# One cost in a scheduling planner: what a one-pass matrix product is reckoned at

## The chip, the cores and the metric

The kernel runs on one core of a Trainium2 chip. The metric is the device time of one execution in microseconds. Before the change the median of three runs was 756.35 us, from 755.69 to 757.19. The profile is of one execution of its own, which took 755.57 us; its trace spans 753.8 us from the first instruction to the last.

The core has five engines that matter here. TensorE (PE) multiplies matrices, and loads the stationary operand in a pipeline beside it (PEld). VectorE (DVE) and ScalarE (ACT) work element by element, GpSimd (POOL) does a few small things, and SyncE (SP) starts the transfers. Each engine takes its instructions strictly in the order in which they were written, so an instruction that waits holds up everything behind it on its engine.

## The reference

One layer of a transformer-like trunk over 512 positions of width 1024, in float32:

```python
h = token_mixer(rmsnorm(x, norm_mix_pre), w_in, b_in, ...) ; x = x + rmsnorm(h, norm_mix_post)
h = memory_cross_attention(rmsnorm(x, ...), rmsnorm(mem, ...), wq, wk, wv, wo) ; x = x + rmsnorm(h, ...)
h = conv_glu_ffn(rmsnorm(x, ...), w_up, conv_w, conv_b, w_down) ; x = x + rmsnorm(h, ...)
```

The token mixer projects the normed rows with w_in and runs four groups of four heads side by side: an mLSTM in chunks, a short causal convolution, a blockwise attention with a position bias, and a gated linear recurrence (HGRN) in chunks. Their outputs are joined and multiplied with w_out. Cross attention reads 256 memory rows. The feed-forward part has 2816 gated channels with a causal convolution of width 3.

## The kernel before

**Arithmetic.** A float32 product is done in one of two ways. Where it feeds a long sum (all projections, the output matrices, the feed-forward part), both operands are split into a high and a low part of type fp32r, and three products are made of one: high by high, high by low, low by high (`three`, L480). These are the one-pass products. Each reads the moving operand once. Small products inside the recurrence and the attentions stay in plain float32; the trace shows two MATMUL records for each of those.

**Splitting.** `stage` loads a weight tile (tile `st`), ScalarE writes the high part `wh`, VectorE the low part `wl`. `split` (L483) does the same for activations. So each weight and each activation passes both of these engines before TensorE can use it.

**The planner.** No instruction order is written by hand. The program below first only records operations; each has an engine, a cost in ns, the buffers that it reads and writes, and a unit. `schedule` (L209) then plays the program through: for every engine it keeps the time at which the engine is free, `est` (L234) gives the earliest time at which a ready operation could start by the costs and by fixed gaps between engines, and of those that could start within 1 ns of the earliest the one with the longest chain of costs behind it (plus a boost) is taken. The order in which the operations are taken is the order in which they are issued (`issue`), and also decides which buffer each gets. So a cost enters twice: in the clock of the plan and in the length of the chains. It has no part in what an instruction does on the chip.

The cost of a TensorE operation comes from `mcost` (L451), summed over its products by `mms` (L457). For one-pass products before the change it is

```python
return max(n, 2 * m) / 2.4 + 2.4
```

where n is the number of columns and m at most 128. That is 215.7 ns at 512 columns and 109.1 ns at 256 and fewer. Plain float32 products, transposes (109 ns, `tpose`) and the narrow products of `pair` (L473) have prices of their own.

**The stages**, in order of time: loading and norming x; the projection of the mixer with the HGRN, mLSTM and attention groups woven into it; the memory projections; w_mix_out; cross attention; the feed-forward part up (`w_ffn_in`) and down (`w_ffn_out`). The HGRN group is the function `hgrn_tile` (L793). For each of four tiles of 128 positions and two pairs of heads it makes decay exponents on TensorE (`mats` by `lfh`, `lfl`), exponentiates them on ScalarE (tile `E`), multiplies by query and key on VectorE (tiles `Qt` and `E` again, by `kT`), multiplies these on TensorE, and writes the result through masks into `at` on VectorE (L427). A state per pair of heads (`state`) runs through the four tiles. While that chain goes back and forth, TensorE has projections of the same stage to do, which the planner puts between. In the mLSTM group a row of gates (`ra`, `rg`, `rb`) passes ScalarE and VectorE before TensorE transposes it (`p_322`).

Of the kernel before, what the change touches and what calls it, by code (L numbers as in the profile page):

```python
# [341 lines left out]
def kernel(  # L342
# [108 lines left out]
    def mcost(l, n):  # L451
        m = min(l.size(), P)
        if l.buf.dt == FR:
            return max(n, 2 * m) / 2.4 + 2.4
        return max(n, m) / 0.6 + 4.8

    def mms(o, terms, first=True, last=True, spare=0, n=None, quota=(), after=(), boost=0.0, fifo=None, cold=1):  # L457

        def go():
            for j, (l, r) in enumerate(terms):  # L460
                i = nc.tensor.matmul(o.ap(), l.ap(), r.ap(), start=first and j == 0,  # L461
                                     stop=last and j == len(terms) - 1)
            return i
        return pl.op("PE", cold * sum(mcost(l, n or o.size()) for l, r in terms), go,
                     reads=[v for t in terms for v in t] + ([] if first else [o]), writes=[o], spare=spare, quota=quota, after=after, boost=boost,
                     fifo=fifo if first else None)
# [453 lines left out]
    for h in range(4):  # L920
        with pl.unit():
# [3 lines left out]
            for i in range(NT):  # L925
                n = S - i * P
# [32 lines left out]
    for g in range(2):  # L959
# [6 lines left out]
        for j in range(NT):  # L966
            with pl.unit():
                js, n = slice(j * P, (j + 1) * P), (j + 1) * P
# [342 lines left out]
```

## Time and profile before

| | |
|---|---|
| median of three runs | 756.35 us (755.69 to 757.19) |
| profiled execution, its own time | 755.57 us |
| its span in the trace | 753.8 us |
| TensorE busy | 741.5 us, 98% of the span |
| VectorE busy | 419.4 us, 56% |
| ScalarE busy | 336.8 us, 45% |
| chain that ended last | PE 95%, DVE 2%, DMA 1% |
| HBM traffic | 75.0 MB read, 2.1 MB written |

The chain that ended last is followed back from the last instruction, at each step to what released it. It is TensorE for 95% of the span. Busy time of TensorE overstates its work, because the ends of its pipelined products are modelled; the distance from one start to the next is the better measure. The averages hide that VectorE is busy nearly all of one stretch, and less than half of another.

### The profile page before, as it was taken

How to read it: one execution, taken by the hardware profiler on the slowest of the kernel's cores; microseconds unless marked ns; L12 is line 12 of the kernel's file. 1: busy time of each engine (PE TensorE's matmuls, PEld its weight loads, DVE VectorE, ACT ScalarE, POOL GpSimd, SP SyncE). 2: the span in 40 equal slices, each digit the busy share in tenths (PEclk: the TensorE clock that was granted, in tenths of full speed). 3: DMA queues.
4: the chain of work that ended last, by engine and by line, in shares of the span. 5: the costliest groups of instructions: out<-in, count | busy, mean ns of one | idle time of the engine just before them, and what ended most of it. 6: DMA issues, size and time to landing. Idle time of an engine off the chain costs nothing.

```text
span 753.8 us, 10351 instructions
## 1 busy us (share of the span) xinstructions
PE 741.5 (98%) x4038; PEld 631.1 (84%) x4038; DVE 419.4 (56%) x799; ACT 336.8 (45%) x662; POOL 35.5 (5%) x65
## 2 busy tenths in 40 slices
PE   7999999999999999999999999999999999999996
PEld 6899989998888988989888888888888888888885
DVE  4879948777664745596755443554344453234005
ACT  5794438437663643485635323344232343123002
POOL 3000210030000000000100000000000000000001
PEclk9999999999999999999999999999999999999998
DMA  8801220500515632243232232223132233245002
GB/s 294 299 1 52 79 92 28 197 29 29 197 57 183 221 126 85 85 140 113 90 107 86 82 93 75 85 85 94 46 111 68 73 88 107 84 167 168 1 0 112
DMA packets 24538, 77.78 MB, mean 103 GB/s; under 512 B 2853, under 2 KB 4517, under 8 KB 24489
## 3 DMA queue, kind: packets, MB, share of 16 engines
q1 hardware_dynamic: 24200, 76.53, 30.7%
q8 instruction: 32, 0.52, 0.3%
q0 software_dynamic: 288, 0.59, 0.3%
q14 instruction: 18, 0.14, 0.1%
HBM read 75.00 MB, written 2.11 MB: 102 GB/s over the span
## 4 chain that ended last, share of the span: by engine, by line
PE 95%; DVE 2%; DMA 1%; SPq 0%; issue 0%; ACT 0%; POOL 0%; DVEq 0%; POOLq 0%; ACTq 0%
PE p L461 91%; PE p L478 3%; DMA st<-in_w_in_dram 1%; PE p L473 1%; DVE at L427 1%; DVE Qt L399 1%; SPq L370 0%; DMA cols<-in_cols_dram 0%; DVE E L399 0%; DVE state L411 0%; DVE xs L411 0%; DVE X L411 0%; DVE xTl L399 0%; POOL rr L564 0%; DVEq L1307 0%
## 5 line engine op out<-in xcount | busy, mean ns | idle before, releaser
L461 PE MATMUL p<-xTh,wh 128*128 128x512 f32 (+1 forms) x560 | 211.8, 378 | 0.2 <-ACT xTh L386 0.2
L461 PE MATMUL p<-xTl,wh 128*128 128x512 f32 (+1 forms) x560 | 210.1, 375 | 0.2 <-DVE xTl L399 0.2
L461 PE MATMUL p<-xTh,wl 128*128 128x512 f32 (+1 forms) x560 | 209.6, 374 | 0.0
L399 DVE TENSOR_TENSOR wl<-st,wh 128x1024 fp32r<-128x1024 f32 (+3 forms) x117 | 138.0, 1194 | 89.2 <-ACT wh L386 74.9
L386 ACT ACTIVATE wh<-st 128x1024 fp32r<-128x1024 f32 (+3 forms) x117 | 117.5, 1031 | 57.7 <-DMA st<-in_w_ffn_out_dram 48.4
L461 PEld LDWEIGHTS p<-xTh,wh 128*128 128x128 f32 x560 | 105.4, 188 | 20.2 <-ACT xTh L386 0.5
L461 PEld LDWEIGHTS p<-xTh,wl 128*128 128x128 f32 x560 | 105.2, 188 | 20.5
L461 PEld LDWEIGHTS p<-xTl,wh 128*128 128x128 f32 x560 | 105.2, 188 | 19.8 <-DVE xTl L399 0.5
L461 PE MATMUL p<-wh,hT 128*128 128x512 f32 x288 | 90.1, 393 | 0.0
L411 DVE SCALAR_TENSOR_TENSOR fc<-p,cols,fc 128x511 f32<-128x511 f32 (+1 forms) x44 | 32.8, 748 | 92.7 <-ACT fc L386 92.0
L461 PEld LDWEIGHTS p<-wh,hT 128*128 128x128 f32 x288 | 54.1, 188 | 12.6
L386 ACT ACTIVATE fc<-p,cols 128x512 f32<-128x512 f32 x22 | 15.0, 684 | 97.9 <-PE p L461 97.9
L461 PE MATMUL p<-wh,xTh 128*128 128x256 f32 (+1 forms) x192 | 56.7, 296 | 0.2 <-ACT xTh L386 0.2
L461 PE MATMUL p<-wl,hT 128*128 128x512 f32 x144 | 56.7, 394 | 0.0
L461 PE MATMUL p<-wh,xTl 128*128 128x256 f32 (+1 forms) x192 | 54.1, 282 | 0.4 <-DVE xTl L399 0.4
L461 PE MATMUL p<-wl,xTh 128*128 128x256 f32 (+1 forms) x192 | 54.0, 281 | 0.0
L399 DVE TENSOR_TENSOR pg<-p,gain 128x512 f32<-128x512 f32 x24 | 16.4, 685 | 52.7 <-ACT sq L386 52.7
L386 ACT ACTIVATE sq<-p 128x512 f32<-128x512 f32 x24 | 14.4, 600 | 67.7 <-PE p L461 67.5
L564 POOL TENSOR_TENSOR rr<-rv,mhalf 128x1 f32<-128x1 f32 x26 | 15.0, 576 | 579.9 <-DVE rv L406 575.4
L461 PEld LDWEIGHTS p<-wh,xTh 128*128 128x128 f32 x192 | 36.3, 189 | 0.9 <-ACT xTh L386 0.5
L461 PEld LDWEIGHTS p<-wh,xTl 128*128 128x128 f32 x192 | 36.2, 188 | 0.6 <-DVE xTl L399 0.6
L461 PEld LDWEIGHTS p<-wl,xTh 128*128 128x128 f32 x192 | 36.2, 189 | 0.5
(236 smaller groups left out, 1085.1 us busy)
## 6 DMA issues: line engine op xcount, KB each, us to landing
st<-in_w_ffn_in_dram SPq DMA_DIRECT2D x44, 512.0 KB, 3.6
st<-in_w_in_dram SPq DMA_DIRECT2D x24, 512.0 KB, 4.7
st<-in_w_ffn_out_dram SPq DMA_DIRECT2D x22, 512.0 KB, 3.6
st<-in_w_mix_out_dram SPq DMA_DIRECT2D x8, 512.0 KB, 3.7
st<-in_w_ck_dram SPq DMA_DIRECT2D x4, 512.0 KB, 5.1
st<-in_w_cv_dram SPq DMA_DIRECT2D x4, 512.0 KB, 5.1
st<-in_w_cq_dram SPq DMA_DIRECT2D x4, 512.0 KB, 4.2
X<-in_x_dram SPq DMA_DIRECT2D x4, 512.0 KB, 5.1
```

The costliest lines, as they stand in the source:

```text
L386: return nc.scalar.activation(o.ap(), i.ap(), func, **kw)
L399: return pl.op(eng, c, lambda: e.tensor_tensor(o.ap(), a.ap(), b.ap(), op=op), reads=[a, b], writes=[o], fifo=fifo, boost=boost)
L411: lambda: nc.vector.scalar_tensor_tensor(o.ap(), a.ap(), ap(s), b.ap(), op0=op0, op1=op1),
L427: return pl.op("DVE", dcost(n, True), lambda: nc.vector.copy_predicated(o.ap(), m.ap(), a.ap()), reads=[m, a, o], writes=[o])
L461: i = nc.tensor.matmul(o.ap(), l.ap(), r.ap(), start=first and j == 0, stop=last and j == len(terms) - 1)
L473: i = nc.tensor.matmul(o[hh * 64:hh * 64 + 64].ap(), l.ap(), r.ap(), start=j == 0, stop=j == len(terms) - 1)
L478: return pl.op("PE", 109.0, lambda: nc.tensor.transpose(o.ap(), a.ap(), idn.ap()), reads=[a, idn], writes=[o])
L564: pl.op("Pool", 470.0, lambda: nc.gpsimd.tensor_tensor(r.all.ap(), v.all.ap(), mhalf[:, :1].ap(), op=OP.pow), reads=[v.all, mhalf.all], wr ...
```

## The change

One line of the cost function is replaced. The price of a one-pass product becomes `max(n, 2 * m) * 0.4445 + 3.7`: 231.3 ns at 512 columns, 174.4 at 384, 121.0 at 264, and 117.5 ns at 256 and fewer. All else of the program text is the same, and so are the instructions in kind and number. What differs is their order on each engine, and the buffers.

```diff
     def mcost(l, n):
         m = min(l.size(), P)
         if l.buf.dt == FR:
-            return max(n, 2 * m) / 2.4 + 2.4
+            return max(n, 2 * m) * 0.4445 + 3.7
         return max(n, m) / 0.6 + 4.8
```

In the orders below a name has the buffer's own number first and then its place in the issue order; the first is the same in both programs, the second is not. The first TensorE row that differs is the 47th, a product of the forget gate's projection about 21 us into the run.

TensorE at the end of the HGRN group. `p_249` is the last of the products that take a `Qt` and an `E` from VectorE; `p_113` and `p_116` are a projection for which `wh_108` holds the first half of the weights and `wh_111` the second. Before:

```order
L461 MATMUL p_113_1009<-wh_111_564,xTh_11_63 128x256
L461 MATMUL p_113_1009<-wl_112_578,xTh_11_63 128x256
L461 MATMUL p_113_1009<-wh_111_564,xTl_12_64 128x256
L461 MATMUL p_249_1152<-Qt_248_1132,E_247_1122 128x128 x2
L461 MATMUL p_249_1152<-Qt_248_1132,kT_228_844 128x128
L461 MATMUL p_250_1160<-hqb_88_75,kT_228_844 128x256
```

Now:

```order
L461 MATMUL p_116_1111<-wh_108_457,xTh_11_63 128x256
L461 MATMUL p_116_1111<-wl_109_467,xTh_11_63 128x256
L461 MATMUL p_116_1111<-wh_108_457,xTl_12_64 128x256
L461 MATMUL p_249_1132<-Qt_248_1107,E_247_1091 128x128 x2
L461 MATMUL p_249_1132<-Qt_248_1107,kT_228_823 128x128
L461 MATMUL p_250_1136<-hqb_88_75,kT_228_823 128x256
```

`p_249` has moved ahead of the second half of that projection. Counted over the whole order, 27 one-pass products that stood ahead of it now stand behind it (6 of 512 columns into `p_266`; 12 into `p_113` and 9 into `p_116`, of 256), and 3 plain products of `p_239` have come ahead of it.

VectorE just ahead of the operations that feed `p_249`. Before:

```order
L411 SCALAR_TENSOR_TENSOR state1_105_83<-state1_105_83,gl_219_1044,p_217_996 64x64
L399 TENSOR_TENSOR ho_129_826<-ho_129_826,rr_155_1065 128x256
L399 TENSOR_TENSOR wl_278_1124<-st_276_778,wh_277_780 128x1024
L399 TENSOR_TENSOR Qt_248_1132<-E_247_1122,hqb_88_75 128x128 x3
L399 TENSOR_TENSOR E_247_1122<-E_247_1122,kT_228_844 128x256
```

Now:

```order
L427 COPY_PREDICATED at_230_957<-masks_55_238,p_239_1052 128x256
L411 SCALAR_TENSOR_TENSOR state1_105_83<-state1_105_83,gl_219_1069,p_217_982 64x64 x2
L399 TENSOR_TENSOR hv_91_580<-p_102_818,bbc_92_309 128x256
L444 TENSOR_REDUCE hss_153_1102<-hsq_152_1063 128x4
L399 TENSOR_TENSOR Qt_248_1107<-E_247_1091,hqb_88_75 128x128 x3
L399 TENSOR_TENSOR E_247_1091<-E_247_1091,kT_228_823 128x256
```

From `Qt_137` (the first operation of the second half of HGRN tile 0) to `E_247`, three operations have moved behind (`wl_278`, `ho_129`, `rv_154`) and six have moved ahead (four into `at_230`, `Qp_240`, one into `hv_91`).

TensorE and ScalarE in the mLSTM gates. `p_318` and `p_317` are transposes of the gate inputs, `p_272` and `p_284` projections. TensorE before:

```order
L461 MATMUL p_272_1316<-xTh_11_63,wl_271_1060 128x512
L478 MATMUL p_318_1505<-ident_7_88,mif_286_1483 4x128 x2
L478 MATMUL p_317_1503<-ident_7_88,mif_286_1483 4x128 x2
L461 MATMUL p_284_1592<-xTh_11_63,wh_282_895 128x512
L461 MATMUL p_284_1592<-xTl_12_64,wh_282_895 128x512
```

and now:

```order
L461 MATMUL p_272_1300<-xTh_11_63,wl_271_876 128x512
L461 MATMUL p_284_1582<-xTh_11_63,wh_282_999 128x512
L461 MATMUL p_284_1582<-xTl_12_64,wh_282_999 128x512
L461 MATMUL p_284_1582<-xTh_11_63,wl_283_1168 128x512
L478 MATMUL p_318_1501<-ident_7_88,mif_286_1483 4x128 x2
L478 MATMUL p_317_1499<-ident_7_88,mif_286_1483 4x128 x2
```

Three products have come ahead of the transposes. Behind them 24 products of 512 and 12 of 256 columns stood ahead of `p_322`; now 21 and 6 do. ScalarE there, before:

```order
L386 ACTIVATE pz_267_1589<-p_272_1316,cols_57_254 128x512
L386 ACTIVATE ra_319_1598<-p_318_1505 4x512
L386 ACTIVATE pH_268_1603<-pz_267_1589 128x512
L386 ACTIVATE ra_319_1598<-ra_319_1598 4x512
L386 ACTIVATE hh_258_1611<-pH_268_1603 64x512
L386 ACTIVATE ra_319_1598<-ra_319_1598,one_10_92 4x512
```

and now:

```order
L386 ACTIVATE pz_267_1580<-p_272_1300,cols_57_254 128x512
L386 ACTIVATE pH_268_1597<-pz_267_1580 128x512
L386 ACTIVATE ra_319_1605<-p_318_1501 4x512
L386 ACTIVATE hh_258_1610<-pH_268_1597 64x512
L386 ACTIVATE ra_319_1605<-ra_319_1605 4x512
L386 ACTIVATE hh_258_1610<-pH_268_1597 64x512
L386 ACTIVATE ra_319_1605<-ra_319_1605,one_10_92 4x512
```

The third step of `ra` now has one more copy (`hh_258`) ahead of it. On VectorE the two copies into `hh_258`, which stood between the three later steps of `ra`, have moved ahead of them.

## Rows read from the trace of the kernel before

**Rows 1.** The page: instructions and span, then busy us of each engine.

```profile
span 753.8 us, 10351 instructions
PE 741.5 (98%) x4038; PEld 631.1 (84%) x4038; DVE 419.4 (56%) x799; ACT 336.8 (45%) x662; POOL 35.5 (5%) x65
```

**Rows 2.** Windows: stretch; length; busy of PE, PEld, DVE, ACT, POOL; clock; DMA; GB/s.

```profile
48.00:66.00 18.00, 18.00 (x141) 17.19 (x140) 17.44 (x65) 12.66 (x34) 0.94 (x3) 1.00 0.00 1
66.00:93.00 27.00, 26.68 (x198) 24.87 (x198) 26.63 (x95) 11.12 (x35) 4.34 (x4) 1.00 0.27 90
386.00:747.00 361.00, 361.00 (x1582) 293.37 (x1581) 144.00 (x167) 110.16 (x143) 1.65 (x3) 1.00 0.27 84
```

**Rows 3.** PE timeline, one-pass products: start, length (us), instruction, idle and releaser.

```profile
82.44 0.28 PE L461 MATMUL p<-wl,xTh 128*128 128x256 f32 x1
82.56 0.28 PE L461 MATMUL p<-wh,xTl 128*128 128x256 f32 x1
82.94 0.46 PE L461 MATMUL p<-Qt,E 128*128 128x128 f32 x2
...
384.89 0.49 PE L461 MATMUL p<-xTh,wh 128*128 128x512 f32 x1 [0.25 <-ACT xTh L386]
...
450.27 0.39 PE L461 MATMUL p<-xTh,wh 128*128 128x512 f32 x1
450.50 0.39 PE L461 MATMUL p<-xTl,wh 128*128 128x512 f32 x1
```

**Rows 4.** PE timeline around the last HGRN products.

```profile
66.38 0.28 PE L461 MATMUL p<-wh,xTl 128*128 128x256 f32 x1
66.89 0.49 PE L461 MATMUL p<-Qt,E 128*128 128x128 f32 x2 [0.23 <-DVE E L399]
...
87.24 0.67 PE L461 MATMUL p<-Qt,E 128*128 128x128 f32 x4
...
89.46 0.38 PE L461 MATMUL p<-state,Qp 128*128 128x128 f32 x2
...
90.05 0.36 PE L461 MATMUL p<-wh,xTh 128*128 128x256 f32 x1
```

**Rows 5.** DVE timeline ahead of the last HGRN products.

```profile
84.91 1.22 DVE L399 TENSOR_TENSOR wl<-st,wh 128x1024 fp32r<-128x1024 f32 x1
86.05 0.69 DVE L399 TENSOR_TENSOR Qt<-E,hqb 128x128 f32<-128x128 f32 x3
86.66 0.42 DVE L399 TENSOR_TENSOR E<-E,kT 128x256 f32<-128x256 f32 x1
87.11 1.04 DVE L427 COPY_PREDICATED at<-masks,p 128x128 f32<-128x128 uint8 x4
87.95 0.32 DVE L399 TENSOR_TENSOR Qp<-E,hq 128x128 f32<-128x128 f32 x1
```

**Rows 6.** ACT timeline early in the HGRN group.

```profile
53.56 1.09 ACT L386 ACTIVATE E<-p 128x512 f32<-128x512 f32 x2 [0.98 <-PE p L461]
```

**Rows 7.** Timelines of the mLSTM gates: PE, ACT and DVE.

```profile
132.10 0.28 PE L461 MATMUL p<-wh,xTl 128*128 128x256 f32 x1
132.31 0.22 PE L478 MATMUL p<-ident,ra 4*128 4x4 f32 x1
...
127.25 0.63 ACT L386 ACTIVATE hh<-pH 64x512 fp32r<-64x512 f32 x1
127.90 0.72 ACT L386 ACTIVATE ra<-ra,one 4x512 f32<-4x512 f32 x1
...
129.37 0.41 DVE L423 CAST hh<-pH 64x512 fp32r<-64x512 f32 x1
130.94 0.42 DVE L423 CAST hh<-pH 64x512 fp32r<-64x512 f32 x1
```

**Rows 8.** PE timeline, change from one-pass products to narrow ones and back.

```profile
192.18 0.44 PE L473 MATMUL p<-pt,av 128*64 128x128 f32 x4
192.55 0.50 PE L461 MATMUL p<-hh,hl 128*128 128x512 f32 x1
```

## Prediction

> **What bounds the kernel now.** I read the page's busy times first. TensorE is busy for 741.5 of 753.8 us [rows 1], and the other engines for little more than half or less. So the end is set by the sum of what TensorE has to do and the moments in which it waits. The change leaves its products as they are in kind and number; it can only move waits and the small costs between unlike products.
>
> Next I asked whether the new price is nearer to the truth, in TensorE's timeline. Starts, not lengths, are to be compared, since the ends are modelled. Two one-pass products of 512 columns start at 450.27 and 450.50, 0.23 us apart; two of 256 start at 82.44 and 82.56, 0.12 apart [rows 3]. The new prices are 231.3 and 117.5 ns, the old ones 215.7 and 109.1. The trace thus shows the new price as the true one, within the two digits of the rows, at a clock of 1.00 [rows 2]. A page of the Trainium skill speaks for the old price: "TensorE: Matmul & The Clock Gate", section "Wait — 56ns, not 53.3ns?", gives N/2.4 plus about 2.5 ns from start to start, 215.7 ns at 512 columns. By that figure the old plan kept true time and the new one makes TensorE too slow; the trace does not agree (0.23 us), and I reckon with the trace.
>
> Then I looked by windows for where TensorE waits at all. From 386 to 747 us it is busy in all of 361.00 us [rows 2], so there is nothing to win there. From 48 to 66 us VectorE is busy for 17.44 of 18.00 us and from 66 to 93 us for 26.63 of 27.00 us [rows 2]. That is the HGRN group, and there VectorE and TensorE are both nearly full. TensorE's waits in it are seen in the timeline: 66.38 to 66.89 is 0.51 where a 256-column product takes 0.12, so 0.39 of wait for `E` [rows 4]; 82.56 to 82.94 is 0.38, so 0.26 [rows 3]. The two make 0.65; with several of about 0.1 each I estimate 1.5 us of waits between 66 and 91 us. One other wait is plain, 0.25 us at 384.89 for an `xTh` of ScalarE [rows 3], at a place where the order has not changed, so it stays. All that better ordering can win is therefore some 1.5 us in the HGRN group and a few tenths elsewhere. What it can lose has no such limit.
>
> **The change part by part.** The one thing removed or added is a price. What it moves is read from the orders, what that costs from the rows.
>
> *The end of the HGRN group.* In the old order the last products that need a `Qt` and an `E`, `p_249`, start at 87.24 [rows 4], and the `E` they read is finished on VectorE at 86.66 + 0.42 = 87.08 [rows 5]. So they came just in time: 0.16 us after it, with no slack. In the new order TensorE reaches them with less work behind it: 27 one-pass products now stand behind `p_249`, 6 of 512 and 21 of 256 columns, which is 6 x 0.23 + 21 x 0.12 = 1.38 + 2.52 = 3.90 us. Three plain products of `p_239` have come ahead, from 89.46 to 90.05 = 0.59 us [rows 4]. So TensorE arrives 3.90 - 0.59 = 3.3 us earlier.
>
> Does VectorE deliver earlier by as much? From `Qt_137` to `E_247` its order has lost `wl_278` (84.91 to 86.05, 1.14 us [rows 5]) and two small operations, and gained four copies into `at` (87.11 to 87.95, 0.84 us for four, [rows 5]), a `Qp` and a gating product of `hv`, each of a few tenths. These cancel within about 0.2 us. VectorE is full in this stretch, so it delivers earlier only if it begins earlier. That can be: the first products of the group (`p_134`) have 18 products of 256 columns and two transposes fewer ahead of them, 18 x 0.12 = 2.2 us and some 0.1, about 2.3 us; and early in the group ScalarE waited for TensorE's exponents, 0.98 us at 53.56 [rows 6]. What of the 2.3 reaches the end of the chain no row shows: nothing if VectorE's other work is what fills it, all of it if the exponents were what it lacked. I take 1.0, by the nearest row, ScalarE's 0.98. So the added wait is 3.3 - 1.0 = 2.3, less 0.1 for slack left at 87.08: +2.2 us. Its ends are 3.3 - 2.3 - 0.1 = +0.9, and 3.3 - 0.1 = +3.2. What stands behind the waiting `p_249` on TensorE is the projection into `p_113` and `p_116`, ready long before: work that was used as cover is simply done later and costs the same, so the wait is pure loss. Should VectorE be less late than I think, the 1.5 us of present waits could go as well, which makes the lower end of this term -1.5.
>
> This is also the mechanism that I believe in. The old price let the plan's TensorE run ahead of the real one by 7 in 100. In the plan, then, TensorE arrived at such places too early, and the planner put filling work ahead of them; on the chip this surplus of filler covered VectorE and ScalarE where those are later than their own prices say. With the true price for TensorE alone that surplus is gone.
>
> *The mLSTM gates.* `p_322` starts at 132.31, 0.21 after a product of 256 columns at 132.10 [rows 7], so it already waits 0.09 us: no slack there either. Of its filler, 24 products of 512 and 12 of 256 columns behind the transposes, 21 and 6 are left. The three of 512 now stand before the transposes and move those as well, so measured from the end of `p_272` TensorE comes 6 x 0.12 = 0.7 us earlier. The chain of `ra` has on ScalarE one copy of `hh` more ahead of its third step, 127.25 to 127.90 = 0.65 us, and on VectorE two copies of `hh` fewer between its steps, 0.41 + 0.42 = 0.83 us [rows 7]; the difference is -0.2. The added wait is 0.7 - 0.2 = +0.5 us; the ends are 0, if the copies that moved had already been hidden by a wait for ScalarE, and 0.7 + 0.65 = 1.35 less 0.1, about 1.2, if VectorE gives nothing back.
>
> *Between unlike products.* Narrow products of `pair` cost something at the change to and from one-pass ones. From 192.18 to 192.55 are 0.37 us for four records of 128 columns [rows 8]; at the pace of 512 columns in 0.23 us they would need 4 x 0.058 = 0.23, so a return to one-pass products costs about 0.15. The new order has three more such returns and two fewer entries, which I take at something under 0.1 each: 0.45 - 0.2, some +0.2 us, from 0 to 0.5.
>
> *Elsewhere.* In the attention, in cross attention and in the feed-forward part the distances from producer to consumer are kept or the chains are shorter by an operation. TensorE has no wait to lose there from 386 us on, and other work of its own to do when a chain is late. I take 0, from 0 to 0.5. SyncE's transfers come in nearly the same order; none of the waits above is for one.
>
> The sum is 2.2 + 0.5 + 0.2 + 0 = +2.9 us. Against the profiled execution that is 755.57 + 2.9 = 758.5 us. The median of the runs shown lies 0.8 above that execution, and on it the forecast is 756.35 + 2.9 = 759.2 us.
>
> **The rivals.**
>
> *The start is earlier by all that TensorE gives it* (no change). If VectorE's chain begins 2.3 us sooner and the wait at the gates is hidden by its copies, 0.9 + 0 + 0.1 remain: 757.3 us. For it speaks ScalarE's wait of 0.98 us, which shows that the exponents were late; against it, that VectorE was busy for 97 in 100 of the stretch at the same time [rows 2], so that little of its lateness came from waiting.
>
> *The true price puts the work where it is needed* (faster). With TensorE's clock right the plan sees which products come too late for VectorE's next step, and places them earlier; the 1.5 us of waits in the HGRN group go, the 0.09 at the gates goes, and two fewer entries save some 0.2: 756.35 - 1.8 = 754.6 us. It decides if VectorE starts more than 3.3 us earlier, or if its operations between `Qt_137` and `E_247` wait less than now. For it speaks that the exponents and first products do stand earlier; against it, that VectorE has only 0.37 us of idle time in 66 to 93 us to give, so it must gain before 66 us, where it has 0.56 [rows 2].
>
> *The attention loses its cover too* (slower still). There, too, filler was placed by the false price. If the upper end of the first term holds and 0.5 for the attention, 0.5 for the changes and 0.7 at the gates come to it, the sum is 3.2 + 0.5 + 0.5 + 0.7 = +4.9: 761.3 us. Against it speaks that no wait is seen there now.
>
> *The price tells nothing at all.* The first 46 TensorE instructions and the whole of the down projection stand as before, and TensorE's sum of products is fixed; if waits only change places, the time stays at 756.4. I count it to the first rival.
>
> **How the numbers follow.** A measurement of this kernel can tell about 0.2% from no change, 1.5 us: 754.8 to 757.9. I give my forecast 0.51 (its own range 757.9 to 760.3, from the ends of its first term with the middle of the others), slower still 0.09, the two cases of no change 0.28, faster 0.12. Slower is then 0.51 + 0.09 = 0.60. The range from 755.4 to 761.2 leaves out the faster case and the upper part of the last, not quite 0.2.
>
> **What would show it right or wrong.** In the profile after, TensorE's busy time should be about the same and the span longer by some 3 us. The first step is right if `p_249` starts 0.2 us or less after the end of its `E`, while TensorE's last product before it started over 1 us earlier, and if the operation `E` ends between 1 and 3 us late against TensorE's own work. It is wrong if the whole stretch of HGRN, reckoned by the TensorE work done up to `p_249` and not by the clock, ends with less waiting than before: then VectorE began sooner than I took. The second step is right if `p_322` shows 0.3 us or more of idle time released by VectorE's `ra`, wrong if it follows the product before it without a gap. If there are waits of more than 0.5 us after 140 us, the "elsewhere" is wrong. If the time is below 755 us, the mechanism itself is: the surplus of filler was not what covered VectorE.

## The result and the profile after

The changed kernel takes 761.97 us (median of four runs, 761.11 to 762.78) against 756.02 us of the kernel before on the same chip: 1.0078 times as long, 95% interval 1.0058 to 1.0098. That is 5.95 us slower. The forecast was 759.2 us, with 761.2 as its upper end: the direction is right, the size half of what came. The profiled execution took 761.11 us.

The page and the windows of the changed kernel (stretch; length; busy of PE, PEld, DVE, ACT, POOL; clock; DMA; GB/s), to be held against [rows 1, 2]:

```profile
span 759.3 us, 10365 instructions
PE 746.2 (98%) x4038; PEld 632.2 (83%) x4038; DVE 418.9 (55%) x799; ACT 336.3 (44%) x662; POOL 34.9 (5%) x65
...
48.00:66.00 18.00, 17.85 (x129) 16.09 (x128) 17.62 (x64) 11.00 (x31) 0.94 (x3) 1.00 0.00 1
66.00:93.00 27.00, 26.59 (x198) 24.54 (x198) 25.52 (x91) 10.06 (x30) 4.58 (x5) 1.00 0.27 90
386.00:747.00 361.00, 360.53 (x1589) 292.62 (x1588) 142.30 (x166) 110.14 (x142) 1.65 (x3) 1.00 0.26 83
```

Neither the number of products (4038) nor the clock (1.00) has changed. The span is 5.5 us longer. VectorE and ScalarE do the same work in all. PE's busy time is up by 4.7 us although it does the same products: a modelled end often hides a wait, so busy time is no way to find the loss. What finds it is to take the n-th product of each trace and to subtract its start in the trace before. At the numbers below, the same work lies behind TensorE in both kernels, to within three products of the same size (us against the kernel before; the last two columns are experiments, the first one below and the one with the lower price; in them up to seven 256-column products stand in place of small transposes at number 900):

```
 product      before   after  true small ops   price below
     100       20.68   +0.04           +0.38         -0.21
     850      131.29   +2.09           -0.24         +0.22   end of HGRN and what follows
     900      137.28   +2.84           -0.10         +0.41   the mLSTM gates
    1175      181.45   +2.73           -0.29         +1.73   mLSTM
    1500      225.90   +4.11           -0.26         +1.70   the attention
    2450      384.04   +4.75           +0.28         +4.30   cross attention
    4025      744.33   +5.52           +0.66         +4.50   the feed-forward part
```

So the 5.5 us are 2.1 to the end of HGRN, 0.75 at the gates, 1.4 in the attention, 0.6 in cross attention and 0.8 in the feed-forward part, less 0.1 in the mLSTM. The offset at product 100 comes from the start-up and is no part of this: two executions of one kernel differ there by 0.5 us (the changed kernel: +0.04 and -0.45) and by 0.85 us (the fastest kernel: +0.80 and -0.05). The waits themselves, in TensorE's timeline of the changed kernel (start, length, instruction; in brackets idle time and what released it):

```profile
61.85 0.27 PE L461 MATMUL p<-wh,xTl 128*128 128x256 f32 x1
62.18 0.35 PE L461 MATMUL p<-Qt,E 128*128 128x128 f32 x1
...
75.85 0.27 PE L461 MATMUL p<-wh,xTl 128*128 128x256 f32 x1
76.38 0.68 PE L461 MATMUL p<-Qt,E 128*128 128x128 f32 x4 [0.25 <-DVE E L399]
...
86.23 0.28 PE L461 MATMUL p<-wh,xTl 128*128 128x256 f32 x1
86.35 0.38 PE L461 MATMUL p<-Qt,E 128*128 128x128 f32 x2
...
133.49 0.28 PE L461 MATMUL p<-wh,xTl 128*128 128x256 f32 x1
134.42 0.22 PE L478 MATMUL p<-ident,ra 4*128 4x4 f32 x1 [0.65 <-DVE ra L399]
...
190.29 0.27 PE L461 MATMUL p<-wh,xTl 128*128 128x256 f32 x1
190.71 0.79 PE L478 MATMUL p<-ident,pr 128*128 128x128 f32 x3
...
333.99 0.40 PE L461 MATMUL p<-wl,oh 128*128 128x512 f32 x1
334.74 0.50 PE L461 MATMUL p<-wh,ol 128*128 128x512 f32 x1 [0.35 <-DVE ol L399]
```

Less 0.12 us for a product of 256 columns (0.23 for 512), the steps are waits of 0.21, 0.41, 0, 0.81, 0.30 and 0.52 us. Between 48 and 85 us there are eleven of 0.13 to 0.41, 2.3 us together; before the change there were four, 1.0 us together, and [rows 3, 4] hold the two largest. The rest of the loss to the end of HGRN lies in smaller steps. The third pair is `p_249`, where the forecast put its main wait: there is none. `E` for it on VectorE:

```profile
85.54 0.42 DVE L399 TENSOR_TENSOR E<-E,kT 128x256 f32<-128x256 f32 x1
```

It ends at 85.96 and not at 87.08 as in [rows 5], and TensorE comes at 86.35.

### The profile page after: what moved, and what is told of

It reads as the page before. It is cut to its first block, busy times and chain, and to the rows that moved or that the text cites. A ratio compares the mean times of both kernels' runs of the same rounds, so it can differ in the third digit from the quotient of the medians.

```text
span 759.3 us, 10365 instructions
## 1 busy us (share of the span) xinstructions
PE 746.2 (98%) x4038; PEld 632.2 (83%) x4038; DVE 418.9 (55%) x799; ACT 336.3 (44%) x662; POOL 34.9 (5%) x65
## 4 chain that ended last, share of the span: by engine, by line
PE 90%; DVE 4%; ACT 3%; DMA 1%; issue 1%; POOL 0%; SPq 0%; DVEq 0%; POOLq 0%; ACTq 0%
PE p L461 86%; PE p L478 3%; DMA st<-in_w_in_dram 1%; PE p L473 1%; ACT wh L386 1%; DVE at L427 1%; DVE Qt L399 0%; ACT e L386 0%; DVE E L399 0%; ACT hqb L386 0%; DVE lo L399 0%; ACT f L386 0%; ACT ra L386 0%; DVE wl L399 0%; POOL rr L564 0%
## 5 line engine op out<-in xcount | busy, mean ns | idle before, releaser
L461 PE MATMUL p<-xTh,wh 128*128 128x512 f32 (+1 forms) x560 | 211.6, 378 | 0.2 <-ACT xTh L386 0.2
L461 PE MATMUL p<-xTl,wh 128*128 128x512 f32 (+1 forms) x560 | 210.5, 376 | 0.2 <-DVE xTl L399 0.2
L461 PE MATMUL p<-xTh,wl 128*128 128x512 f32 (+1 forms) x560 | 209.8, 375 | 0.0
L461 PEld LDWEIGHTS p<-xTh,wh 128*128 128x128 f32 x560 | 105.2, 188 | 20.7 <-ACT xTh L386 0.5
L461 PEld LDWEIGHTS p<-xTh,wl 128*128 128x128 f32 x560 | 105.2, 188 | 20.6
L461 PEld LDWEIGHTS p<-xTl,wh 128*128 128x128 f32 x560 | 105.3, 188 | 19.8 <-DVE xTl L399 0.5
L461 PE MATMUL p<-wh,hT 128*128 128x512 f32 x288 | 90.2, 394 | 0.0
L461 PEld LDWEIGHTS p<-wh,hT 128*128 128x128 f32 x288 | 54.1, 188 | 12.5
L461 PE MATMUL p<-wh,xTh 128*128 128x256 f32 (+1 forms) x192 | 56.5, 294 | 0.2 <-ACT xTh L386 0.2
L461 PE MATMUL p<-wl,hT 128*128 128x512 f32 x144 | 56.6, 393 | 0.0
L461 PE MATMUL p<-wh,xTl 128*128 128x256 f32 (+1 forms) x192 | 54.0, 281 | 0.4 <-DVE xTl L399 0.4
L461 PE MATMUL p<-wl,xTh 128*128 128x256 f32 (+1 forms) x192 | 54.1, 282 | 0.0
L461 PEld LDWEIGHTS p<-wh,xTh 128*128 128x128 f32 x192 | 36.3, 189 | 1.0 <-ACT xTh L386 0.5
L461 PEld LDWEIGHTS p<-wh,xTl 128*128 128x128 f32 x192 | 36.2, 188 | 0.6 <-DVE xTl L399 0.6
L461 PEld LDWEIGHTS p<-wl,xTh 128*128 128x128 f32 x192 | 36.2, 189 | 0.4
```

## The experiments

**What the plan gets wrong.** With the true TensorE price I looked for operations of the other engines that take longer from one to the next than the planner's costs (lines 370 to 430) say. In ScalarE's and VectorE's timelines of the changed kernel, first the one and then the other:

```profile
52.60 1.21 ACT L386 ACTIVATE at<-p 64x128 f32<-64x128 f32 x6
53.84 0.38 ACT L386 ACTIVATE kT<-p 128x256 f32<-128x256 f32 x1
...
129.59 0.63 ACT L386 ACTIVATE ra<-ra 4x512 f32<-4x512 f32 x1
130.25 0.63 ACT L386 ACTIVATE hh<-pH 64x512 fp32r<-64x512 f32 x1
```

```profile
77.87 0.57 DVE L411 SCALAR_TENSOR_TENSOR state<-state,gl,p 64x64 f32<-64x64 f32 x2
78.47 0.42 DVE L399 TENSOR_TENSOR hv<-p,bbc 128x256 f32<-128x256 f32 x1
...
132.37 1.21 DVE L416 TENSOR_TENSOR_SCAN rg<-ra 4x512 f32<-4x512 f32 x1
133.69 0.68 DVE L399 TENSOR_TENSOR ra<-p,rg 4x512 f32<-4x512 f32 x1
```

Six copies into `at` take 1.24 us. Two of them (64 partitions, 128 elements) are priced at 159 ns and start 0.16 apart; that leaves 0.92 / 4 = 0.23 us for each of the four into 32 partitions, which the plan prices at 105 ns. A step of `ra` takes 0.66 (price 0.52), two state updates 0.60 (price 0.38), a scan 1.32, or 1.14 at the least (price 0.605). The large operations are priced to a hundredth: `E` by `kT` with 512 columns is priced at 0.605 and takes 0.60 from its start to the next. So the plan takes VectorE's and ScalarE's chains for earlier than they are, just where they are made of small steps. The plan's own times show it: from the first products of the HGRN group (`p_134`) to the last (`p_249`) the changed kernel's plan reckons 33.8 us, and the chip takes 37.5.

Theory A starts from there. The old TensorE price was 7% low. It let TensorE run through its work faster than it can, so that more of it was put ahead of the chains' products, and made up for that. Rival B is that a slower TensorE in the plan does harm by itself, rival C that any other price draws another order at random.

**All small operations priced as measured, TensorE's new price kept:**

```diff
+        rows = o.box[0][1] - o.box[0][0]
+        if rows < (64 if i.buf.cls == "P" else P):
+            extra += 104.0 if i.buf.cls == "P" else 122.0
...
-        return pl.op("DVE", dcost(n or o.size(), True) + 60.0,
+        return pl.op("DVE", dcost(n or o.size(), True) + 60.0 + 110.0 * (o.box[0][1] - o.box[0][0] == 64),
...
-        return pl.op("DVE", dcost(o.size(), True),
+        return pl.op("DVE", 62.0 + 2.1 * o.size(),
```

(Cut from the whole edit. The last is the scan; likewise 100 ns more for VectorE's copies and 95 for its operations on two tiles, both of 512 columns on part of the partitions, 62 for a scaling by a column, 40 for the two coarser masked copies.)

> The new TensorE price, and beside it the small operations of ScalarE and VectorE priced at the distances seen in the traces (a ScalarE copy into 32 partitions of at 209 ns instead of 105, copies of 512 columns on part of the partitions 641 instead of 519 on ScalarE and 432 instead of 333 on VectorE, the scans 1135 instead of 605, the state update about 300 instead of 190). Theory A, that the low TensorE price had paid for these low prices: the waits before TensorE's Qt-E products, the 0.8 us before the transpose of ra and those before the transposes of pr go, about 1.8 + 0.7 + 0.5 = 3 us or more, so 757 to 759 us, with the wait of 0.5 us before wh-ol in cross attention left. Rival B, that a slow TensorE in the plan is harmful by itself, whatever the others cost: about 762 us as in the changed kernel. Rival C, that any change of a price draws another order at random: any time from 756 to 764, with waits at new places.

Measured: 755.63 us, 0.9993 of before (0.9984 to 1.0002). The whole loss is gone, more than A had claimed (757 to 759); B is out. The plan now reckons 36.6 us from `p_134` to `p_249`, and the chip takes 37.6. The gates, in TensorE's timeline of this kernel (its lines stand three lower, so L464 is L461):

```profile
132.58 0.28 PE L464 MATMUL p<-wh,xTl 128*128 128x256 f32 x1
132.79 0.22 PE L481 MATMUL p<-ident,ra 4*128 4x4 f32 x1
...
329.48 0.39 PE L464 MATMUL p<-wl,oh 128*128 128x512 f32 x1
330.29 0.50 PE L464 MATMUL p<-wh,ol 128*128 128x512 f32 x1 [0.42 <-DVE ol L402]
```

0.21 us from the product to the transpose of `ra`, as before the change [rows 7], and not 0.93. The wait in cross attention stays: 0.81 - 0.23 = 0.58.

**The same with the old TensorE price** (`mcost` as before the change, all small operations as measured).

> The same true prices of ScalarE and VectorE, with the old TensorE price (215.7 ns). Theory A: TensorE is covered even more, so no slower than before, 755 to 757 us, and the waits of 0.1 to 0.4 us before Qt-E products near 66, 78 and 83 us shrink. Rival B: the old price alone decides, 756 us with the waits unchanged. Rival C: any time, as likely 760 as 756.

Measured: 754.58 us, 0.9975 (0.9965 to 0.9984), faster than before. Measured a second time:

> The fastest version so far once more, true prices of ScalarE's and VectorE's small operations with the old TensorE price. If its lead is real: 0.1 to 0.35% faster than before (1.7 us at the first time), and 6.5 to 8 us faster than the changed kernel. If it was the chip or the draw of runs: within 0.1% of before.

Measured: 754.14 us, 0.9977 (0.9968 to 0.9986). The lead holds; against the changed kernel in the same comparison it is 7.5 us. This is the version to take. It is also 1 us faster than the kernel in which every price is the measured one, and A does not say why.

**The price halfway, and one step below the old one** (`max(n, 2 * m) * 0.43055 + 3.05`, and `* 0.3889 + 1.1`).

> The TensorE price halfway, 223.5 ns at 512 columns and 113.3 at 256, all else as in the changed kernel. Theory A and rival B: the cover goes gradually, half of the loss, about 759 us (757.5 to 760.5), with part of the waits at ra, pr and Qt-E. Rival C: not between the two, below 756 or above 762.

> The TensorE price one step below the old one, 200.2 ns at 512 columns and 100.7 at 256. Theory A in its plain form and rival B: more cover still, so 756 us or a little less. Rival C, or a form of A in which cover beyond the need does harm (a chain's step that is ready stands behind filler on TensorE, so the next engine gets it late): slower, 757 us or more.

Measured: 756.92 us for halfway (1.0011, 1.0002 to 1.002) and 760.19 for the lower one (1.0056, 1.0042 to 1.007). Neither A in its plain form nor B holds: halfway brings 0.7 of the 5.95 us and not half (its trace has waits of the same kinds, 0.36 us before `rg` at the gates and 0.16 before `pr`), and a still lower price costs 3.9 us. TensorE's timeline with the lower price:

```profile
57.61 0.28 PE L461 MATMUL p<-wh,xTl 128*128 128x256 f32 x1
58.38 0.35 PE L461 MATMUL p<-Qt,E 128*128 128x128 f32 x1 [0.48 <-DVE E L399]
...
152.96 0.28 PE L461 MATMUL p<-lo,hl 128*128 128x256 f32 x1
154.43 0.36 PE L461 MATMUL p<-hh,hl 128*128 128x256 f32 x1 [1.20 <-ACT W L386]
...
330.38 0.41 PE L478 MATMUL p<-ident,cpr 128*128 128x128 f32 x2 [0.63 <-ACT cpt L386]
```

There the waits are at other places: 1.35 us before an mLSTM product that waits for a `W` of ScalarE (which had itself waited 2.24 us for a transfer of `mp`), and in cross attention, where 2.6 of the 4.5 us are lost. So a lower price is harmful as well; that filler stood ahead of a ready step there was not read from the order. A is kept in this form: what counts is the proportion of TensorE's price to those of the chains beside it, and the old price was near it by two errors of opposite sign. That is an argument and not a result: the kernel with all small prices measured and the old TensorE price has TensorE too fast in proportion, and is the fastest. C would allow such times, but not that the loss of a stage comes and goes with the prices of that stage, which is the next test.

**The small prices in two parts:** HGRN's alone (copies into 32 partitions of `at`, state updates, masked copies), and the others alone, each with the new TensorE price.

> The new TensorE price, and of the true prices only those of the HGRN group: the copy into 32 partitions of at 104 ns more, the state update of 64 partitions 110 more, the masked copies of the two coarser levels 40 more. Theory A says that each group's waits hang on its own prices: the waits between 48 and 91 us go as in the first run (1.8 us), the 0.8 us before ra at 133 us and the waits before pr near 190 us stay, and the 0.5 us in cross attention: 762.0 - 1.8 = about 760 us (759 to 760.8). Rival: the order after 100 us is settled by what went before, and recovers as well: 756 to 757. Rival: the HGRN prices do nothing alone: 762.

> The other part alone: the copies of 512 columns on part of the partitions, the scans, the scaling of pr; the HGRN prices as in the changed kernel. Theory A: the waits before ra and pr go (0.8 + 0.5 us and the dearer changes near 200 us, together some 2 to 2.5), those between 48 and 91 us stay: 762.0 - 2.3 = about 759.7 (758.5 to 761). Rival, all or nothing: 756 or 762.

Measured: 759.14 us (1.004, 1.0028 to 1.0052) and 759.36 us (1.0044, 1.0031 to 1.0058). Each takes away its own part. With the HGRN prices the shift at product 850 is +0.6 instead of +2.1 us (+0.49 of it already at product 100), and the 0.75 us at the gates (0.49 of it in the step shown first) and the 1.4 us of the attention (from +1.43 to +2.79) stay. With the others it is the reverse: from +1.62 to +1.72 at the gates and from +1.52 to +1.57 in the attention, and most of what HGRN loses now stands in one wait, at an instruction that had none in the changed kernel. So the prices of a stage decide its loss, but not at which instruction it falls. The six times of the second kernel form two groups, 757.9 to 758.4 us at a granted clock of 0.998 and 760.3 to 760.7 at 0.993; the trace is of the first, so at the higher clock its loss is nearer to 2.5 us than to the median's 3.6. TensorE's timeline, first of the one, then of the other kernel:

```profile
132.36 0.28 PE L464 MATMUL p<-wh,xTl 128*128 128x256 f32 x1
132.97 0.22 PE L481 MATMUL p<-ident,ra 4*128 4x4 f32 x1 [0.33 <-DVE ra L402]
```

```profile
66.65 0.28 PE L464 MATMUL p<-wh,xTl 128*128 128x256 f32 x1
68.74 0.46 PE L464 MATMUL p<-Qt,E 128*128 128x128 f32 x2 [1.81 <-DVE E L402]
```

**The new price in one half of the program.** A flag gives the new price up to and with `w_mix_out` and the old one after, then the reverse:

```diff
+    slow = [True]
...
-            return max(n, 2 * m) * 0.4445 + 3.7
+            return max(n, 2 * m) * 0.4445 + 3.7 if slow[0] else max(n, 2 * m) / 2.4 + 2.4
...
+    slow[0] = False
     pl.boost = 0
     wq = [stage(wsrc(w_cq, r * 2, 2, 0, 512), [P, 2, 512], 9) for r in range(4)]
```

> The new TensorE price only for the products up to and with w_mix_out, the old one from the projection of cross attention on; all other prices as in the changed kernel. Theory A: the loss sits in the mixer, but for the wait of 0.51 + 0.1 us before wh-ol in cross attention, which goes: 762.0 - 0.6 = about 761.4 (760.4 to 761.7). Rival, that the rest of the loss (some 0.7 us that the changed kernel's profile shows to come little by little in the feed-forward part) hangs on the price there: 760.7 or less. Rival, that it is the price of the later products that does the harm: 757.

> The counterpart of the kernel with the new price in the mixer alone (4.4 us slower): the old price up to and with w_mix_out, the new one from the projection of cross attention on. If the losses of the two halves add up to the whole: 5.95 - 4.4 = 1.5 us slower, of which 0.6 are the wait before wh-ol in cross attention and up to 0.75 the growth in the feed-forward part. If only the wait belongs to the price: 0.6 us slower. If the halves work on each other: 0, or over 2.

Measured: 760.22 us (1.0054, 1.0042 to 1.0066) and 756.58 us (1.0012, 1.0003 to 1.0021): 4.4 and 0.6 us slower, together 5.1 against 5.7 to 5.95 for both. The second has its loss in one wait before `wh,ol` (0.42 us, from 330.39 to 331.04 less 0.23). The first came out where "the rest hangs on the price in the feed-forward part" had put it, 1.2 us below A's 761.4; but with the new price there alone nothing of the growth came (see below).

**All true prices in the mixer, the old TensorE price from cross attention on** (the flag in the first experiment).

> All true prices in the mixer (TensorE's and the small operations'), and the old TensorE price from cross attention on. Theory A with the two losses added up: the first run's 755.6 less its wait of 0.58 + 0.1 us before wh-ol in cross attention: about 754.9, faster than before by 0.1 to 0.3%. Rival, that the wait moves to another place of cross attention: 755.6 as in the first run.

Measured: 755.32 us, 0.9997 (0.9988 to 1.0005), no change that can be told. The wait before `wh,ol` is gone, but one of 0.31 + 0.23 us before and among the transposes of `ho` at 101 us has come, in a stretch whose prices are those of the first experiment. Its order on TensorE parts from that of the first experiment at 73 us already: since a chain's length counts what comes behind it, a price late in the program moves work early in it too.

**The changed kernel again.**

> The changed kernel once more, beside the next two on the same chip. If the first measurement (5.95 us over before) was typical: 5.3 to 6.5 us slower than before, and in the profile the waits at the same instructions (0.8 us before ra, 0.5 before wh-ol). Of the slow growth in the feed-forward part (230.59 ns from one product to the next against 230.09 before, some 0.75 us in all): if it belongs to the price, it comes again (230.3 or more); if it belonged to that execution, 230.1 or less may come.

Measured: 761.64 us, 1.0083 (1.0068 to 1.0097), with the same waits at the same instructions, to 0.01 us. The feed-forward part came out with 230.59 ns from product to product again.

**How A fared.** Of the eight times that A forecast here, two came in its ranges, those of the two parts. The first two experiments came out faster than it said; halfway, the lower price, the new price in the mixer and the last mixture missed as well. A gives the stage of a loss, and not its size.

## Why the prediction was too small

*That the new price is the true one and the change makes the kernel slower:* right. *The mechanism* (the surplus of a plan in which TensorE is too fast covers VectorE and ScalarE, which are later than their own prices): borne out. Measured prices for the small operations take the whole loss away, those of one stage the loss of that stage, and the plan's time for the HGRN chain goes from 33.8 to 36.6 us where the chip takes 37.5 and 37.6. The forecast could not say which prices were false; they were the small operations'. That the loss follows the surplus in proportion is not shown: halfway lost about an eighth, a lower price lost again, and the kernel with the small prices and the old TensorE price won.

*The end of HGRN, +2.2 us (0.9 to 3.2):* measured 2.1. VectorE delivered the last `E` 1.1 us earlier, where I had taken 1.0. That was luck in part, since the 1.0 was taken from a row that had no tie to the end of the chain. And the wait is not at `p_249`: the 3.3 us of filler were gone from the whole group, and eleven small waits before it had already held TensorE back. The sign that I named for this step (`p_249` 0.2 us or less behind its `E`) failed, since it starts 0.39 behind; the sum held.

*The gates, +0.5 us (0 to 1.2):* measured 0.81 - 0.09 = 0.72. The -0.2 us for the chain was wrong. ScalarE's and VectorE's steps, before the change and after it:

```profile
125.02 0.69 ACT L386 ACTIVATE pz<-p,cols 128x512 f32<-128x512 f32 x1 [0.75 <-PE p L461]
...
128.76 0.68 DVE L411 SCALAR_TENSOR_TENSOR ra<-p,ra 4x512 f32<-4x512 f32 x1
...
131.40 0.68 DVE L399 TENSOR_TENSOR ra<-p,rg 4x512 f32<-4x512 f32 x1
```

```profile
127.08 0.69 ACT L386 ACTIVATE pz<-p,cols 128x512 f32<-128x512 f32 x1 [0.77 <-PE p L461]
...
130.90 0.72 ACT L386 ACTIVATE ra<-ra,one 4x512 f32<-4x512 f32 x1
...
130.28 0.86 DVE L423 CAST hh<-pH 64x512 fp32r<-64x512 f32 x2
131.65 0.68 DVE L411 SCALAR_TENSOR_TENSOR ra<-p,ra 4x512 f32<-4x512 f32 x1 [0.51 <-ACT ra L386]
```

From `pz`, which waits for `p_272`, to the third step of `ra` (127.90 in [rows 7]) ScalarE takes 3.82 us and not 2.88: +0.94, where I had 0.65 for the added copy. The way from there to VectorE's first step is 0.11 shorter, and that from VectorE's first step to its last (133.69 above) 2.04 us and not 2.64: the moved copies give back 0.60 and not 0.83. So the chain is 0.23 longer, not 0.2 shorter. And `p_322` had some slack before: it started 0.91 us after the start of that last step, now 0.73. 0.7 + 0.23 - 0.18 = 0.75, as in the table.

*Between unlike products, +0.2 us (0 to 0.5):* about +0.4. There are seven returns to one-pass products instead of four, as counted. At all eleven places of both traces 0.20 us lie between the last narrow product and the one-pass one, where a transpose leaves 0.03; that is 0.17 each (I had 0.15 from [rows 8]), together 0.52. The entries and the exits to transposes cost 0.09 each; the two fewer entries from one-pass products were made up by three more from transposes, which I had not counted, and there are two exits to transposes fewer: 0.52 - 0.19 + 0.28 - 0.18 = 0.43.

*Elsewhere, 0 (0 to 0.5):* this is the step that failed. It came to 0.9 + 0.6 + 0.8 = 2.3 us. In the attention TensorE waits before the transposes of `pr` (0.29 and 0.19 us) and of `xs` (0.19), 0.67 in all; with the 0.43 of the step above, 0.3 of the 1.4 us are left, in steps of 0.1 and less. I had argued that no wait is seen there now. That shows only that the old order had cover, not how much; the order should have been counted for it as it was at HGRN and at the gates. In cross attention the step from `wl,oh` to `wh,ol` had no wait before. The same two places before the change, 0.12 and 0.24 us from start to start:

```profile
188.96 0.28 PE L461 MATMUL p<-wh,xTl 128*128 128x256 f32 x1
189.08 0.71 PE L478 MATMUL p<-ident,pr 128*128 128x128 f32 x5
...
330.00 0.40 PE L461 MATMUL p<-wl,oh 128*128 128x512 f32 x1
330.24 0.39 PE L461 MATMUL p<-wh,ol 128*128 128x512 f32 x1
```

The rival that named the attention was right about the place, and the chance of 0.09 was too small. That its 761.3 us came so near is luck: 3.2 of its 4.9 us were the upper end of HGRN, which came to 2.1, and it had neither the 0.6 of cross attention nor the 0.8 of the feed-forward part.

*The feed-forward part, from 386 us on nothing:* wrong by 0.8 us, and not by a single wait: no distance there reaches 0.3 us. The 1505 distances between TensorE's products 2520 and 4025, in the kernel before and the changed one:

```profile
398.05 0.39 PE L461 MATMUL p<-xTh,wh 128*128 128x512 f32 x1
...
744.33 0.63 PE L461 MATMUL p<-xTh,hT 128*128 128x512 f32 x2
```

```profile
402.81 0.39 PE L461 MATMUL p<-xTh,wh 128*128 128x512 f32 x1
...
749.85 0.63 PE L461 MATMUL p<-xTh,hT 128*128 128x512 f32 x2
```

346.28 and 347.04 us, 230.09 and 230.59 ns on average. The changed kernel has 230.59 in both its profiled executions, the fastest kernel 229.79 in both of its, the kernel with the new price from cross attention on 230.08. It belongs to the program, then, and not to the execution or the price in that part. The order isn't quite the one before: by their buffers, 453 of these 1506 products stand at other places (six of them in the down projection, of which I had said that it stays). But the order alone is not the cause either. The kernel with the new price from cross attention on has in this part the order of the changed kernel on every engine, and 230.08 ns. What differs between these two is the places of the buffers (252 of 304; between the kernel before and the changed one 274) and what came before. Whether the places are the cause wasn't tried; it stays open.

## What to carry to other kernels

A planner's prices work together: setting one of them to its measured value in a plan where others are false can cost more than the error did (5.95 us here), so measure the small operations on the chains that wait too, and then time the mixtures, since the fastest here kept one false price. Where an engine shows no wait, count the cover in the old and the new order before pricing its loss at nothing. And hold two traces against each other by the n-th product of the engine that is full, not by busy time.

## What was not expected of the hardware

ScalarE's copies of 64 elements into 32 partitions start 0.21 to 0.24 us apart, those of 128 elements into 64 partitions 0.16 to 0.17. A scan of 512 columns on 4 partitions takes 1.14 to 1.32 us from its start to the next, where an element by element operation on two tiles of that length takes 0.60 to 0.70. And one program has the same mean distance of its products to a hundredth of a ns in two executions, while another with the same products in the same order differs by 0.5 ns (230.59 and 230.08).
